# Making the right operands of the second layer's Strassen products during the first layer, by way of DRAM

## The chip, the core and the metric

The kernel runs on one core of one Trainium2 chip. The time is that of one execution on the device in microseconds (us); a run's time is that of the core. PE is TensorE (the matmuls), DVE is VectorE, ACT is ScalarE, POOL is GpSimd, and SP is SyncE, which here only issues DMAs.

## What is computed

One layer of an encoder, batch 1, 2048 positions, width 1024, all in float32. Three mixers (dilated attention, latent attention, spatial gating) and an output projection come first and are not touched. The part that matters here is the MLP behind them:

```python
x = _layer_norm(ALPHA * x + y @ w_out, ln1_g, ln1_b)
f = jnp.square(jax.nn.relu(x @ w_ff1 + b_ff1)) @ w_ff2 + b_ff2      # 1024 -> 4096 -> 1024
return _layer_norm(ALPHA * x + f, ln2_g, ln2_b)
```

## The kernel before, in words

**Numbers.** A float32 operand is split into a high part (a copy to fp32r, on ACT) and a low part (the operand less the high part, on DVE or POOL). A product is then three matmuls, high by high, low by high and high by low (`mm3`, lines 149 to 151). A page is 128 partitions by 512 floats, 256 KB.

**Strassen.** Both layers of the MLP (`feed_forward`) take blocks two by two and make seven products from sums and differences of the blocks. The products are numbered 1 to 7. Each needs a left operand (made by `left`) and a right one (made by `right`); both make the sum or difference first and split it then (`parts`, lines 1367 and 1368).

**Rounds.** A round is the seven products, 84 matmuls of 512 columns, for one pair of blocks. Rounds 0 to 31 are the first layer ("hidden rounds": two halves `hf` of the positions by 16 chunks `c` of the hidden features; left operands W from `w1`, right operands X from the normed x, made once per half). Rounds 32 to 63 are the second layer (8 blocks `c` of the hidden features by 4 groups `g` of positions; left operands H from the hidden features, right operands V from `w_ff2`, made once per block `c` and used in its four rounds). In the second layer each product ends in two additions of a PSUM bank to the result `acc` in SBUF (line 1594, on DVE).

**Order.** `feed_forward` writes the program in the order run a product of round r, prepare the operand of the same number for round r + 1 (`prepare`), and loads what round r + 2 needs at the end of round r. A scheduler then orders each engine's queue. In the hidden rounds PE takes the products of round k in the order 1, 5, 2, 6, 3, 7, 4, with 7 of round k standing between 1 and 5 of round k + 1, and 4 between 5 and 2 of round k + 1. So product 2 of round k + 1 starts right behind product 4 of round k, and its left operand (W..2h and W..2l; the name holds half, chunk and product) is made on ACT and POOL just ahead of it.

**V before.** For each block `c`, four double pages of `w_ff2` are loaded (line 1572), and during the last round of the block before, `right` makes V: 8 subtractions, four on POOL and four on DVE (line 1428), 14 high parts on ACT and 14 low parts on DVE (line 1368). The V pages are held once, not twice: a page is written anew as soon as the product that read it is done. For block 0 this happens in hidden round 31.

**DMA.** All these DMAs are issued by SP, in its queue's order; each waits for its operands and for the DMA eight places ahead of it to have landed.

Of the kernel before, what the change touches and what calls it, by code (L numbers as in the profile page):

```python
# [94 lines left out]
def f(ap):  # L95
    return ap.bitcast(F32)
# [3 lines left out]
def hybrid_layer(ctx: ExitStack, tc: tile.TileContext, a):  # L100
# [33 lines left out]
    y_d = [[dt_([P, TB], f"y_d{i}_{b}") for b in range(NB)] for i in range(8)]  # L134
    x1T_d = [dt_([P, KD, S // 2], f"x1T_d{i}") for i in range(2)]
    xb_d = [dt_([TB, DM], f"xb_d{i}") for i in range(NB)]
    hid_d = [[dt_([P, 4, TB], f"hid_d{i}_{j}") for j in range(NB)] for i in range(8)]

    def hp(k):
# [1213 lines left out]
    def feed_forward(done):  # L1353

        with ExitStack() as es:
# [31 lines left out]
            def load_page(kind, src, nm, view=None):  # L1387
                t = page(kind, nm)
                dma(t if view is None else t.rearrange("p (k c) -> p k c", c=view), src)
                return t  # L1390
# [27 lines left out]
            def right(B, n, nm, late):  # L1418

                out = {}  # L1420

                def put_(p, raws):
                    kind = {1: "X1", 2: "X2", 4: "xr" if n == 2 else "X4"}.get(p, "X")
                    out[p] = [parts(kind, raws[i], f"{nm}{p}{i}", dve) for i in range(n)]

                def sub(o, x, y):
                    for i in range(n):
                        (dve if i % 2 else pool).tensor_tensor(o[i], x[i], y[i], op=ALU.subtract)  # L1428

                def p5():  # L1430
                    sub(B[0, 0], B[0, 1], B[0, 0])
                    put_(5, B[0, 0])

                def p6():
                    sub(B[0, 0], B[1, 1], B[0, 0])
                    put_(6, B[0, 0])

                def p7():
                    sub(B[0, 1], B[1, 1], B[0, 1])
                    put_(7, B[0, 1])  # L1440
                    late()

                def p4():
                    sub(B[0, 0], B[1, 0], B[0, 0])
                    put_(4, B[0, 0])

                return out, {1: lambda: put_(1, B[0, 0]), 5: p5, 6: p6, 3: lambda: put_(3, B[1, 1]), 7: p7,
                             2: lambda: put_(2, B[1, 0]), 4: p4}
# [18 lines left out]
            def hidden_round(hf, c, big, bf1):  # L1467
# [60 lines left out]

                return load, preps, run

            def second_rounds():


                acc, late, gb = {}, [], {}
                rounds = []
                for c in range(DFF // TB):
                    big = {}
                    for g in range(4):
                        rounds.append(second_round(c, g, big, acc, late, gb))
                return rounds, late  # L1540

            def second_round(c, g, big, acc, late, gb):
                nm = f"{c}_{g}"
                end = c == DFF // TB - 1
                A, bks = {}, {}
                H, prep = left(A, "wc", f"H{nm}", (3, 7, 2, 4), {2: "ht", 4: "ht"})
                preps = [prep]
                if g == 0:
                    big["B"] = {}
                    big["W"], bp = right(big["B"], 2, f"V{c}", lambda: None)  # L1550
                    preps.insert(0, bp)
                if c == 0 and g == 0:

                    order = []
                    for q in range(4):
                        for j, n in ((0, 0), (1, 1), (0, 1), (1, 0)):
                            order += [(4 * q + 2 * j + i, n) for i in range(2)]

                    def residual(lo, hi):
                        for m, n in order[lo:hi]:  # L1560
                            acc[m, n] = load_page({0: "X1", 20: "X2", 24: "X4"}.get(lo, "X"), xb_d[m // 4][(m % 4) * P:(m % 4 + 1) * P, n * TB:(n + 1) * TB], f"acc{m}{n}")
                    preps.append({p: (lambda i=i: residual(4 * i, 4 * i + (8 if i == 6 else 4)))
                                  for i, p in enumerate((1, 5, 6, 3, 7, 2, 4))})

                def load():
                    for j in range(2):
                        for k in range(2):
                            A[j, k] = load_page("wr", hid_d[c][g][:, 2 * k:2 * k + 2, 256 * j:256 * j + 256], f"A{nm}{j}{k}", 256)
                    if g == 0:
                        for k, b in ((0, 0), (0, 1), (1, 1), (1, 0)):  # L1570
                            r0 = (4 * c + 2 * k) * P
                            big["B"][k, b] = [load_page("xr", a["w_ff2"][r0 + i * P:r0 + (i + 1) * P, b * TB:(b + 1) * TB],
                                                        f"B{c}{k}{b}{i}") for i in range(2)]
                    if end and g == 1:
                        gb["g"] = row_pages("xr", a["ln2_g"], "g2")
                        gb["b"] = row_pages("xr", a["ln2_b"], "b2")

                sums, norms = {}, []

                def run(p, bk):  # L1580
                    for i in range(2):
                        if p in FRESH:
                            bks[bk, i] = (first_bank(f"o{nm}{p}{i}") if bk == "a" else
                                          bank(dict(b=("av", "st")[i], c="st")[bk], f"o{nm}{p}{i}"))
                        ps = bks[bk, i]
                        for kt in range(2):
                            cols = slice(256 * kt + P * i, 256 * kt + P * i + P)
                            w = big["W"][p][kt]
                            mm3(ps, H[p][0][:, cols], H[p][1][:, cols], w[0], w[1], p in FRESH and kt == 0, kt == 1, True)
                        j, n = {1: (0, 0), 5: (1, 1), 6: (0, 1), 3: (0, 1), 7: (1, 1), 2: (0, 0), 4: (1, 0)}[p]  # L1590
                        m = 4 * g + 2 * j + i
                        t = acc[m, n]
                        if not end or p not in (3, 7, 2, 4):
                            dve.tensor_tensor(t, ps, t, op=ALU.add)  # L1594
                            continue
                        if g == 3:

                            dve.tensor_tensor(t, ps, t, op=ALU.add)
                            if m not in sums:
                                sums[m] = sm.tile([P, 2, 6], F32, tag="stats", name=f"fs{m}", bufs=4)  # L1600
                            dve.bn_stats(sums[m][:, n], t)
                        else:
                            if m not in sums:
                                sums[m] = sm.tile([P, 2], F32, tag="sums", name=f"fs{m}", bufs=4)
                            dve.scalar_tensor_tensor(t, ps, 1.0, t, ALU.mult, ALU.add, accum_out=sums[m][:, n:n + 1])  # L1605
                        if p == ((3 if j == 0 else 4) if end and g == 3 else 2 if j == 0 else 4):
                            def store(m=m):
                                for n in range(2):
                                    dma(a["out"][m * P:(m + 1) * P, n * TB:(n + 1) * TB], acc[m, n])
                            norms.append(layer_norm([acc[m, 0], acc[m, 1]], sums[m], gb["g"], gb["b"], f"b{m}", lambda nm: page("sx", nm), store, dve if m >= 14 else pool,  # L1610
                                                    sums[m] if g == 3 else None))
                    if norms and (len(norms) == 4 or g == 3):
                        n = len(norms)
                        for i in range(n + 2):
                            late.extend(norms[i - k][k] for k in range(3) if 0 <= i - k < n)
                        norms.clear()

                return load, preps, run
# [41 lines left out]
                prepare(2, p)  # L1660
            rounds[3][0]()
            final = len(rounds) - 1
            for r in range(2, len(rounds)):
                for i, (p, bk) in enumerate(LAST if r == final else ORDER):
                    rounds[r][2](p, bk)
                    prepare(r + 1, (LAST if r + 1 == final else ORDER)[i][0])
                    for _ in range(3 if r == final else 2):
                        if late and (i < 6 or r == final):
                            e = late.pop(0)
                            if e:  # L1670
                                e()
                if r + 2 < len(rounds):
                    rounds[r + 2][0]()
# [76 lines left out]
```

## Time and profile before

| | us |
|---|---|
| median of 3 runs | 2957.93 (2956.33 to 2963.31) |
| the profiled execution, its own time | 2963.83 |
| its span, first to last instruction | 2962.0 |
| PE busy | 2809.6 (95%) |
| DVE busy | 2035.9 (69%) |
| POOL busy | 1567.3 (53%) |
| ACT busy | 1334.3 (45%) |

The hidden rounds take the stretch from about 1625 to 2265 us of the span, the second layer from there to the end. Busy time is the sum over instructions; a busy PE can still be waiting for nothing and run at half its clock, which the granted clock shows (1.00 is the full 2.4 GHz). A row of waits tells which engine waited at which line for which instruction, the sum, how often, and the longest.

### The profile page before, as it was taken

How to read it: one execution, taken by the hardware profiler on the slowest of the kernel's cores; microseconds unless marked ns; L12 is line 12 of the kernel's file. 1: busy time of each engine (PE TensorE's matmuls, PEld its weight loads, DVE VectorE, ACT ScalarE, POOL GpSimd, SP SyncE). 2: the span in 40 equal slices, each digit the busy share in tenths (PEclk: the TensorE clock that was granted, in tenths of full speed). 3: DMA queues.
4: the chain of work that ended last, by engine and by line, in shares of the span. 5: the costliest groups of instructions: out<-in, count | busy, mean ns of one | idle time of the engine just before them, and what ended most of it. 6: DMA issues, size and time to landing. Idle time of an engine off the chain costs nothing. (4 is left out here: it accounts for less than half of the span.)

```text
span 2962.0 us, 38261 instructions
## 1 busy us (share of the span) xinstructions
PE 2809.6 (95%) x12562; PEld 2284.3 (77%) x12562; DVE 2035.9 (69%) x3543; ACT 1334.3 (45%) x2510; POOL 1567.3 (53%) x1227
## 2 busy tenths in 40 slices
PE   9999998999899999998999999989999999999996
PEld 7776877888778878886778788868887777777774
DVE  4246877676787878778677733473337777778899
ACT  4225555556555555456544533443434332232243
POOL 0115556546544554458665544554446666565667
PEclk9999999999999999999999999999999999999998
DMA  5335333235122443114374532333326222222222
GB/s 170 122 130 180 109 112 107 97 116 122 35 55 58 88 86 79 36 37 130 101 234 145 167 107 107 107 128 107 114 104 228 84 69 78 78 86 79 78 72 96
DMA packets 255567, 313.99 MB, mean 106 GB/s; under 512 B 79516, under 2 KB 145788, under 8 KB 254844
## 3 DMA queue, kind: packets, MB, share of 16 engines
q1 hardware_dynamic: 242056, 295.82, 33.2%
q10 hardware_dynamic: 13312, 15.73, 1.5%
q8 instruction: 99, 1.62, 0.2%
q14 instruction: 100, 0.82, 0.1%
HBM read 209.72 MB, written 98.60 MB: 104 GB/s over the span
## 5 line engine op out<-in xcount | busy, mean ns | idle before, releaser
L621 POOL TENSOR_TENSOR pl<-pr,ph 128x512 fp32r<-128x512 f32 x384 | 506.8, 1334 | 438.8 <-ACT ph L619 327.7
L1594 DVE TENSOR_TENSOR acc<-o,acc 128x512 f32<-128x512 f32 x416 | 275.0, 683 | 108.3 <-PE o L151 106.1
L618 ACT ACTIVATE pr<-st 128x512 f32<-128x512 f32 x384 | 228.3, 598 | 182.6 <-PE st L613 171.0
L594 DVE TENSOR_REDUCE m<-mx 128x1 f32<-128x512 f32 x384 | 256.5, 682 | 74.2 <-PE mx L593 72.3
L640 DVE TENSOR_TENSOR acp<-acp,pr 128x512 f32<-128x512 f32 x312 | 215.9, 692 | 53.8 <-ACT pr L618 49.2
L619 ACT ACTIVATE ph<-st 128x512 fp32r<-128x512 f32 x384 | 222.9, 598 | 20.8 <-PE av L647 13.8
L611 PE MATMUL st<-QH,KL 96*128 96x512 f32 x384 | 162.3, 423 | 13.9 <-ACT ph L619 13.1
L593 PE MATMUL mx<-KH,QH 96*128 96x512 f32 x384 | 159.0, 436 | 16.4 <-DVE m L594 9.7
L648 PE MATMUL av<-pl,VV 128*128 128x512 f32 x384 | 161.2, 420 | 6.5 <-POOL pl L621 6.4
L647 PE MATMUL av<-ph,VV 128*128 128x512 f32 x384 | 158.1, 412 | 0.8 <-DVE y L662 0.7
L612 PE MATMUL st<-QL,KH 96*128 96x512 f32 x384 | 154.7, 403 | 0.0
L613 PE MATMUL st<-QH,KH 97*128 97x512 f32 x384 | 154.3, 408 | 0.0
L875 DVE CUSTOM_DVE_ANT_0 jk<-amx,bias 128x256 bf16<-128x256 f32 (+2 forms) x288 | 103.8, 360 | 19.9 <-PE amx L870 10.1
L1521 DVE TENSOR_TENSOR t<-t,h 128x512 f32<-128x512 f32 x32 | 22.0, 686 | 138.4 <-PE h L151 127.0
L1010 PE MATMUL aav<-apr,v 128*65 128x128 f32 (+3 forms) x624 | 113.0, 324 | 2.9 <-DVE acc L998 1.0
L954 PE MATMUL ast<-QB,KB 65*128 65x256 f32 (+1 forms) x288 | 103.6, 372 | 4.9 <-DMA QB<-amr 3.9
L953 PE MATMUL ast<-QA,KA 128*128 128x256 f32 (+1 forms) x288 | 106.3, 374 | 0.9 <-DVE tt L976 0.6
L979 ACT ACTIVATE apr<-tt 128x192 f32<-128x192 f32 (+2 forms) x180 | 77.6, 467 | 62.5 <-PE aav L1010 57.5
L1010 PEld LDWEIGHTS aav<-apr,v 128*65 128x65 f32 x624 | 81.2, 140 | 31.5 <-issue 1.6
L593 PEld LDWEIGHTS mx<-KH,QH 96*128 96x128 f32 x384 | 75.5, 201 | 37.5 <-DVE m L594 16.3
L149 PE MATMUL po<-woh,y 128*128 128x512 f32 x256 | 102.8, 403 | 1.0 <-ACT xT L1266 1.0
L151 PE MATMUL po<-wol,y 128*128 128x512 f32 x256 | 101.9, 400 | 0.7 <-DVE wol L1207 0.7
(9022 smaller groups left out, 8706.3 us busy)
## 6 DMA issues: line engine op xcount, KB each, us to landing
A<-in_w SPq DMA_DIRECT2D x128, 256.0 KB, 2.7
hid_d<-t SPq DMA_DIRECT2D x128, 256.0 KB, 2.7
A<-hid_d SPq DMA_DIRECT2D x128, 256.0 KB, 2.7
B<-in_w_ff SPq DMA_DIRECT2D x64, 256.0 KB, 3.5
xr<-in_xT SPq DMA_DIRECT2D x56, 256.0 KB, 3.5
wr<-in_wf SPq DMA_DIRECT2D x48, 256.0 KB, 3.1
yr<-y_d SPq DMA_DIRECT2D x64, 128.0 KB, 2.3
xt<-in_x SPq DMA_DIRECT2D x32, 256.0 KB, 3.7
```

Source lines behind the costliest of these rows:

```text
L593: pe.matmul(ps, s["QH"][0:96, qt * P:(qt + 1) * P], kh[0:96, kc * TB:(kc + 1) * TB], start=True, stop=True)
L594: dve.tensor_reduce(s["m16"][:, qt, kc:kc + 1], ps, AX.X, ALU.max)
L611: pe.matmul(st, kl[0:96, kk], s["QH"][0:96], start=True, stop=False)
L612: pe.matmul(st, kh[0:96, kk], s["QL"][0:96], start=False, stop=False)
L618: act.activation(pr, st, AF.Exp, scale=SC)
L619: act.activation(ph, st, AF.Exp, scale=SC)
L621: pool.tensor_tensor(pl, pr, f(ph), op=ALU.subtract)
L640: dve.tensor_tensor(s["ac"], old, pr, op=ALU.add)
L647: pe.matmul(s["av"], VV[h][:, kt], ph, start=(kt == 0), stop=False)
L648: pe.matmul(s["av"], VV[h][:, kt], pl, start=False, stop=(kt == NT - 1))
L1010: pe.matmul(s[key][0:65, c0:c0 + w], s["V"][p][:, units[u][2] + j], pr[:, a0:a0 + w], start=(first[key] == i), stop=(last[key] == i), skip ...
L1594: dve.tensor_tensor(t, ps, t, op=ALU.add)
```

## The change

The V operands of all eight blocks are made during the hidden rounds, 16 items of one block `c` and one half `i` each, and stored to DRAM as finished high and low pages (`vv_d`, 14 pages an item). The second layer loads these pages into the V pages as they come free, and makes none of them. An item loads 4 pages of `w_ff2`, makes 4 subtractions (two on POOL, two on DVE), 7 high parts on ACT and 7 low parts on DVE, and stores 14 pages. The program takes it in nine steps, one behind each product, 63 steps from round 2 on and 81 from round 17 on.

```diff
+    vv_d = [[dt_([P, 14, TB], f"vv_d{c}{i}") for i in range(2)] for c in range(DFF // TB)]
...
+            SECOND = (1, 5, 6, 4, 2, 7, 3)
+            def second_right():
+                done_ = []
+                def store():
+                    while done_:
+                        dst, t = done_.pop(0)
+                        dma(dst, t)
+                for c in range(DFF // TB):
+                    for i in range(2):
+                        B = {}
+                        for k, b in ((0, 0), (1, 0), (0, 1), (1, 1)):
+                            r0 = (4 * c + 2 * k + i) * P
+                            B[k, b] = load_page("xr", a["w_ff2"][r0:r0 + P, b * TB:(b + 1) * TB], f"V{c}{i}{k}{b}")
+                        yield
+                        for n, p in enumerate(SECOND):
+                            raw = B[{1: (0, 0), 5: (0, 0), 6: (0, 0), 4: (0, 0), 2: (1, 0), 7: (0, 1), 3: (1, 1)}[p]]
+                            x = {5: (0, 1), 6: (1, 1), 4: (1, 0), 7: (1, 1)}.get(p)
+                            if x:
+                                (pool if p in (5, 4) else dve).tensor_tensor(raw, B[x], raw, op=ALU.subtract)
+                            h = page("xr", f"V{c}{i}{p}h", F32R)
+                            act.copy(h, raw)
+                            l = page("xr", f"V{c}{i}{p}l", F32R) if n < 3 else raw.bitcast(F32R)
+                            dve.tensor_tensor(l, raw, f(h), op=ALU.subtract)
+                            store()
+                            done_.extend([(vv_d[c][i][:, 2 * n], h), (vv_d[c][i][:, 2 * n + 1], l)])
+                            yield
+                        store()
+                        yield
...
-                    big["B"] = {}
-                    big["W"], bp = right(big["B"], 2, f"V{c}", lambda: None)
-                    preps.insert(0, bp)
+                    big["W"] = {}
+                    def fetch(p):
+                        kind = {1: "X1", 2: "X2", 4: "xr"}.get(p, "X")
+                        n = 2 * SECOND.index(p)
+                        big["W"][p] = []
+                        for i in range(2):
+                            hl = [page(kind, f"V{c}_{p}{i}{x}", F32R) for x in "hl"]
+                            for x in range(2):
+                                dma(hl[x], vv_d[c][i][:, n + x])
+                            big["W"][p].append(hl)
+                    preps.insert(0, {p: (lambda p=p: fetch(p)) for p in SECOND})
...
-                    if g == 0:
-                        for k, b in ((0, 0), (0, 1), (1, 1), (1, 0)):
-                            r0 = (4 * c + 2 * k) * P
-                            big["B"][k, b] = [load_page("xr", a["w_ff2"][r0 + i * P:r0 + (i + 1) * P, b * TB:(b + 1) * TB],
-                                                        f"B{c}{k}{b}{i}") for i in range(2)]
...
+            ahead = second_right()
+            quota = [63, 81]
             for r in range(2, len(rounds)):
                 for i, (p, bk) in enumerate(LAST if r == final else ORDER):
                     rounds[r][2](p, bk)
                     prepare(r + 1, (LAST if r + 1 == final else ORDER)[i][0])
+                    if (2 <= r < 12 or 17 <= r < 31) and quota[r // 16]:
+                        quota[r // 16] -= 1
+                        next(ahead)
```

The scheduler decides where the moved work stands. Three places follow.

**DVE, last round of block 0 in the second layer, where V of block 1 was made.** `acc..` are the additions from PSUM, `H..l` and `V..l` low parts of left and right operands, `B..` subtractions for V. Before:

```order
L1368 TENSOR_TENSOR H1_01l_22444<-A1_000_22395,H1_01h_22443 128x512
L1594 TENSOR_TENSOR acc141_21948<-o0_350_22447,acc141_21948 128x512
L1428 TENSOR_TENSOR B1001_22405<-B1011_22409,B1001_22405 128x512
L1368 TENSOR_TENSOR V150l_22466<-B1000_22403,V150h_22465 128x512
L1594 TENSOR_TENSOR acc151_21950<-o0_351_22455,acc151_21950 128x512
L1368 TENSOR_TENSOR H1_05l_22476<-H1_0s_22473,H1_05h_22475 128x512
L1428 TENSOR_TENSOR B1011_22409<-B1111_22413,B1011_22409 128x512
L1594 TENSOR_TENSOR acc121_21952<-o0_310_22419,acc121_21952 128x512
L1368 TENSOR_TENSOR V151l_22470<-B1001_22405,V151h_22469 128x512
L1594 TENSOR_TENSOR acc120_21944<-o0_320_22564,acc120_21944 128x512
```

The same place in the changed program:

```order
L1370 TENSOR_TENSOR H1_01l_23220<-A1_000_23187,H1_01h_23219 128x512
L1635 TENSOR_TENSOR acc141_22740<-o0_350_23223,acc141_22740 128x512
L1635 TENSOR_TENSOR acc100_22704<-o0_210_23050,acc100_22704 128x512
L1635 TENSOR_TENSOR acc110_22706<-o0_211_23058,acc110_22706 128x512
L1635 TENSOR_TENSOR acc151_22742<-o0_351_23231,acc151_22742 128x512
L1370 TENSOR_TENSOR H1_05l_23250<-H1_0s_23247,H1_05h_23249 128x512
L1635 TENSOR_TENSOR acc121_22744<-o0_310_23195,acc121_22744 128x512
L1635 TENSOR_TENSOR acc131_22746<-o0_311_23203,acc131_22746 128x512
L1370 TENSOR_TENSOR H1_06l_23277<-H1_0s_23247,H1_06h_23276 128x512
```

All 18 DVE operations for V are gone from between the additions; only additions and low parts of H are left.

**ACT and POOL, hidden round 3 of the second half, up to the left operand of product 2 of round 4.** `t61_3` and `t71_3` copy a PSUM bank after products 6 and 7, `W1_4..` are left operands of the next round. ACT before:

```order
L1513 ACTIVATE t61_3_19939<-h1_31_19887,bf1_15750 128x512
L1367 CAST W1_46h_19942<-W1_4s_19921 128x512
L1367 CAST W1_43h_19962<-W1_4s_19921 128x512
L1367 CAST W1_47h_19984<-A1_400_19879 128x512
L1513 ACTIVATE t71_3_19978<-h1_31_19887,bf1_15750 128x512
L1367 CAST W1_42h_20004<-A1_401_19881 128x512
```

ACT in the changed program:

```order
L1515 ACTIVATE t61_3_20398<-h1_31_20335,bf1_15766 128x512
L1558 CAST V505h_20754<-V5000_20693 128x512
L1369 CAST W1_46h_20401<-W1_4s_20374 128x512
L1558 CAST V506h_20780<-V5000_20693 128x512
L1369 CAST W1_43h_20426<-W1_4s_20374 128x512
L1369 CAST W1_47h_20450<-A1_400_20327 128x512
L1515 ACTIVATE t71_3_20444<-h1_31_20335,bf1_15766 128x512
L1558 CAST V504h_20807<-V5000_20693 128x512
L1558 CAST V502h_20834<-V5010_20695 128x512
L1558 CAST V507h_20860<-V5001_20697 128x512
L1558 CAST V503h_20885<-V5011_20699 128x512
L1369 CAST W1_42h_20478<-A1_401_20329 128x512
```

POOL in the changed program:

```order
L1410 TENSOR_TENSOR W1_4s_20374<-A1_401_20329,W1_4s_20374 128x512
L1556 TENSOR_TENSOR V5000_20693<-V5010_20695,V5000_20693 128x512
L1520 TENSOR_TENSOR t71_3_20444<-t71_3_20444,t51_3_20372 128x512
L1370 TENSOR_TENSOR W1_42l_20479<-A1_401_20329,W1_42h_20478 128x512
```

Six casts of an item stand among ACT's work, four of them right ahead of W1_42h, and the item's subtraction for product 4 (line 1556) stands ahead of the last two POOL operations before product 2.

**SP, the same last round of block 0 in the second layer.** `A..` are loads of left operands, `V1_..` the new loads, here for products 1 and 5 of block 1:

```order
L145 DMA V1_10h_23211<-vv_d10_142 128x512
L145 DMA V1_10l_23212<-vv_d10_142 128x512
L145 DMA V1_11h_23215<-vv_d11_143 128x512
L145 DMA V1_11l_23216<-vv_d11_143 128x512
L145 DMA A1_200_23533<-hid_d1_2_162 128x2x256
L145 DMA V1_50h_23239<-vv_d10_142 128x512
L145 DMA V1_50l_23240<-vv_d10_142 128x512
L145 DMA V1_51h_23243<-vv_d11_143 128x512
L145 DMA V1_51l_23244<-vv_d11_143 128x512
```

Each V load waits until PE has done the product that reads the page, and loads of left operands stand between them. Product 4's V loads stand earlier, for three blocks at once.

## Rows read from the trace of the kernel before

**Rows 1.** The page's busy time: us, share of the span, instructions.

```profile
PE 2809.6 (95%) x12562; PEld 2284.3 (77%) x12562; DVE 2035.9 (69%) x3543; ACT 1334.3 (45%) x2510; POOL 1567.3 (53%) x1227
```

**Rows 2.** Stretches: length, busy PE, PEld, DVE, ACT, POOL (instructions), clock, DMA share, GB/s.

```profile
1540.00:1560.00 20.00, 20.00 (x98) 16.68 (x97) 12.43 (x29) 9.93 (x25) 10.63 (x12) 1.00 0.97 306
1700.00:1800.00 100.00, 100.00 (x433) 81.05 (x433) 35.31 (x52) 39.59 (x67) 48.57 (x37) 1.00 0.31 110
2270.00:2290.00 20.00, 19.74 (x84) 15.43 (x84) 17.94 (x22) 8.37 (x15) 14.85 (x10) 1.00 1.03 366
2500.00:2600.00 100.00, 95.92 (x411) 76.78 (x410) 83.81 (x106) 32.59 (x57) 62.78 (x45) 1.00 0.22 70
```

**Rows 3.** PE's waits from 2300 to 2880 us: sum, times, longest.

```profile
PE o L149 <- DVE acc L1594: 21.6, 14, 2.5
```

**Rows 4.** Timeline of PE: start, length, instruction, idle time before it and its releaser.

```profile
2517.90 0.50 PE L149 MATMUL o<-V350h,H_05h 128*128 128x512 f32 x1 [0.80 <-DVE acc L1594]
...
2523.66 0.50 PE L149 MATMUL o<-V240h,H_34h 128*128 128x512 f32 x1 [2.48 <-DVE acc L1594]
...
2879.31 0.50 PE L149 MATMUL o<-V730h,H_13h 128*128 128x512 f32 x1 [1.66 <-DVE acc L1594]
```

**Rows 5.** Timeline of a quiet hidden round (round 4), and the first reader of W_52l on PE.

```profile
1710.11 0.69 ACT L1513 ACTIVATE t<-h,bf 128x512 f32<-128x512 f32 x1
...
1729.56 0.69 ACT L1513 ACTIVATE t<-h,bf 128x512 f32<-128x512 f32 x1
1731.83 0.62 ACT L1367 CAST W_52h<-A 128x512 fp32r<-128x512 f32 x1 [1.59 <-PE h L150]
...
1723.73 0.69 DVE L1515 TENSOR_TENSOR t<-t,h 128x512 f32<-128x512 f32 x1 [1.76 <-PE h L151]
...
1732.53 1.29 POOL L1368 TENSOR_TENSOR W_52l<-A,W_52h 128x512 fp32r<-128x512 f32 x1 [0.92 <-ACT W_52h L1367]
...
L150 PE MATMUL h<-X020h,W_52l x1: 389/389/389, 1734.8 to 1734.8; 128*128 128x512 f32 x1
```

**Rows 6.** 2300 to 2860 us: DVE by line; DVE at L1368; DVE and POOL at L1428.

```profile
L1594 DVE TENSOR_TENSOR acc<-o,acc 128x512 f32<-128x512 f32 x382 | 252.4, 683 | 105.8 <-PE o L151 103.7
L1428 DVE TENSOR_TENSOR B<-B,B 128x512 f32<-128x512 f32 x28 | 33.4, 1193 | 0.0
...
2300.00:2860.00 560.00, 185.31 (x181) 1.00 0.24 76
...
2300.00:2860.00 560.00, 33.40 (x28) 39.00 (x28) 1.00 0.24 76
```

**Rows 7.** Timeline of hidden round 31: the first and last operation for V0, POOL's last steps, PE.

```profile
2246.58 0.62 ACT L1367 CAST V010h<-B 128x512 fp32r<-128x512 f32 x1
...
2280.72 1.78 DVE L1368 TENSOR_TENSOR V071l<-B,V071h 128x512 fp32r<-128x512 f32 x1
...
2257.03 1.65 POOL L1428 TENSOR_TENSOR B<-B,B 128x512 f32<-128x512 f32 x1 [1.84 <-PE h L150]
2258.64 1.71 POOL L1368 TENSOR_TENSOR W_152l<-A,W_152h 128x512 fp32r<-128x512 f32 x1
...
2260.40 0.79 PE L150 MATMUL h<-X120h,W_152l 128*128 128x512 f32 x1 [2.96 <-POOL W_152l L1368]
...
2263.55 0.40 PE L151 MATMUL h<-X122l,W_152h 128*128 128x512 f32 x1
```

**Rows 8.** DMA issues: line, operation, count, size, us from issue to landing.

```profile
B<-in_w_ff SPq DMA_DIRECT2D x64, 256.0 KB, 3.5
...
acc<-xb_d SPq DMA_DIRECT2D x32, 256.0 KB, 5.3
```

**Rows 9.** Timeline of ACT and DVE at the start of the hidden rounds.

```profile
1651.36 0.62 ACT L1367 CAST X041h<-x 128x512 fp32r<-128x512 f32 x1
1651.88 0.62 ACT L1367 CAST X022h<-x 128x512 fp32r<-128x512 f32 x1
...
1655.64 1.20 DVE L1368 TENSOR_TENSOR X022l<-x,X022h 128x512 fp32r<-128x512 f32 x1
```

## The prediction

> **What bounds the kernel now.** I read the busy times first, then the stretches, then PE's waits in the stretch that the change is about, and last the timelines of single places. The page says that PE is busy for 95% of the span [rows 1]; so only PE's gaps can be won, some 150 us over the whole kernel, and most of them lie in parts that the change does not touch. The stretches show two different regimes [rows 2]. In the hidden rounds (1700 to 1800) PE is busy without a break, DVE for 35 of 100 us, ACT for 40, POOL for 49, and DMA has a share of 0.31. In the second layer (2500 to 2600) PE is busy for 95.9 and DVE for 83.8. PE's waits name what ends there: 21.6 us of waiting for line 1594, the additions on DVE that free a PSUM bank, and for nothing else [rows 3]. The timeline says when: a gap of 0.80 and one of 2.48 us, close together, once in each block, where the last round of a block meets the first of the next [rows 4]. That is the round in which V is made.
>
> The reason is a sum on DVE. A round lasts 19.45 us (from one copy of a bank to the same copy a round later [rows 5]). In a plain round of the second layer DVE has 14 additions of 0.683 and 3 low parts, together under 13 us. In the round that makes V it has 18 operations more. Line 1368 takes 185.31/181 = 1.02 us each and line 1428 1.19 [rows 6], so these are 14 x 1.02 + 4 x 1.19 = 19.0 us, and with 12.6 for the rest 31.6 us of work for 19.45. What neighbouring rounds don't absorb, PE waits for.
>
> **What the change takes away.** (a) Seven such meetings. The waits are 21.6 us; the last one, 1.66 us at 2879, lies inside block 7 [rows 4], where no V is made, and stays. Gain **19.9 us**. With 17 DVE operations left a round (the DVE rows of the order), DVE is under 13 of 19.45 us, so no addition is late. (b) Hidden round 31. PE waits 2.96 us for W_152l, which POOL reaches late because a subtraction for V0 of 1.65 us stands ahead of it [rows 7]. Behind that gap eight matmuls take 2263.55 - 2260.40 = 3.15 us; at the full clock, 19.45/84 = 0.232 us each, they take 1.85. Gain 2.96 + 1.30 = **4.3 us**. Both bounds for (a) and (b) are near: they are PE's own idle time, and nothing else can be won there.
>
> **What it adds in the second layer.** 28 V loads a block for 8 loads of `w_ff2`. A page is released when its product is done and read a round later, 19.45 us, and a load at full traffic lands after 5.3 us [rows 8]. A round with 28 V loads and some 5 others moves 33 x 0.262 MB = 8.7 MB; at the 366 GB/s that the trace shows [rows 2] that is 23.6 us, 4 more than a round. So the last pages come some 4 + 5 us after their release, 10 ahead of use. I take **nothing**. Behind a V load that waits for PE on SP stand only loads of H's operands, one round or more early. Bounds: 0, and 7 x 5.3 = 37 us if each block waited for one landing.
>
> **What it adds in the hidden rounds.** The order puts about one item into each round, faster than the program's nine steps for seven products: 16 of the 32 rounds carry one. The engines' sums for such a round: ACT 0.40 x 19.45 + 7 x 0.62 = 12.1 us; POOL 0.49 x 19.45 + 2 x 1.39 = 12.3 (1.39 is 39.00/28, POOL's half of line 1428 [rows 6]); DVE 0.353 x 19.45 = 6.9, plus 9 x 1.02 = 9.2, is 16.1, and 18.7 if its own eight SBUF operations also slow from 0.69 to 1.02. All are under 19.45, so no engine is the bound, but the cover on DVE is thin. What counts then is the place with the least lead. That is product 2: ACT writes W_52h at 1731.83, POOL W_52l from 1732.53 to 1733.82, and PE reads it at 1734.8 [rows 5]. The lead is **1.0 us**.
>
> For the round in the order's second place I add up the new chain on the clock of [rows 5]. It starts when DVE adds product 3, 1723.73. Five DVE operations follow up to the low part for product 6 of the item, with a cast between: 5 x 1.02 + 0.62 + 0.7 = 6.4, to 1730.1. POOL's subtraction for product 4, 1.39: 1731.5. The casts V504h to V503h, four at a spacing of 0.52 [rows 9], then W1_42h, 0.62: 1734.2. W1_42l on POOL, 1.29 to 1.71: 1735.5 to 1735.9. That is 0.7 to 1.1 us too late. Without the waits for DVE, four casts behind 1729.56 would delay W1_42h by 0.4 us only, and nothing would be lost. In nine of the 16 rounds POOL's subtraction for product 4 stands ahead of that low part as here; in the other seven it stands behind it or far earlier, and at most two casts stand there: I take 1.0 us for the nine and 0.3 for the seven, **11.1 us**. Below: 0, if operations meet as seldom as in a quiet round. Above: the nearest row of a hidden round with V work in it is round 31, where both items of V0, made from 2246.58 to 2280.72 (1.75 rounds), cost 2.96 us [rows 7], 1.5 an item: 24 us. I stay between, nearer to the chain, since the order around product 2 differs from round 31's.
>
> DVE's 1.78 us for a low part of V [rows 7] against a flat 0.683 for the additions [rows 6] shows what makes V's operations dear: both their inputs lie in SBUF, while an addition has one in PSUM. The Trainium skill says the same in SBUF — State Buffer, Who interferes with whom: a VectorE instruction with two SBUF inputs contends with a GpSimd instruction that reads SBUF, and the later one blocks until the first is done. This rule speaks against the change, which moves 144 such operations next to POOL's work on the operands that PE waits for; the third rival is that rule at its full price.
>
> **Two edges.** At the start, V001h stands on ACT between X041h and X022h [rows 9] and waits for a load issued behind those for X; a load of this kind lands after 3.5 us [rows 8], and X022l on DVE has 3.1 us in hand (1655.64 less 1652.5). I take 2 us, bounds 0 and 5. Where the second half begins, an item mixes into the making of X: 1 us, bounds 0 and 2. Together **3 us**.
>
> **Sum.** -19.9 - 4.3 + 11.1 + 3 = -10.1 us, against the profiled execution's 2963.8: 2953.7. That execution stands 5.9 us above the median of the runs, 2957.9; carried over, **2947.8 us**, 0.34% less. A measurement of this kernel can tell about 0.3%, 8.9 us, from no change, so the forecast is just beyond it. At the lower bounds of all costs: 2957.9 - 24.2 = 2933.7. At the upper bounds of the hidden rounds and the edges: + 24 + 7 - 24.2, 2964.7.
>
> **Rivals.** First, **the gain is given back in the hidden rounds**: product 2 is late by about 1.5 us in every item's round. For it: round 31 did just that. Against it: there, two subtractions stood ahead. Time: 2957.9 - 24.2 + 24 + 3 = 2960.7; with 1 us a round 2953. Both within 0.3%.
>
> Second, **DMA becomes the bound of those rounds**. SP's order holds 24 to 27 DMAs in 13 of them, where it held 8; 26 are 6.8 MB in 19.45 us, 350 GB/s. The trace has 366 at a share of 1.03, and 306 at a share of 0.97 [rows 2]. At 306, 26 take 22.3 us, 2.8 over the round; in 13 rounds that is 37 us: 2957.9 - 24.2 + 37 + 3 = 2973.7. From 323 GB/s downwards (26 in 21.1 us, 1.6 over the round, 21 us in 13) it takes back the whole gain. Against it: the row of 306 lies in another stage, the one of 366 in the rounds next to these, where the same 256 KB pieces move.
>
> Third, on the other side too, **DVE becomes the bound of those rounds**, when V's operations wait for a whole POOL operation each, at 1.78 us: 6.9 + 9 x 1.78 = 22.9 us a round, 3.5 over, 56 us in 16 rounds: 2957.9 - 24.2 + 56 + 3 = 2992.7. It decides once a moved operation takes more than (19.45 - 6.9)/9 = 1.39 us in the mean. Against it: 1.02 and 1.19 in the second layer, with POOL busy for 63 of 100 us there.
>
> Fourth, **V comes late**: PE's wait for DVE becomes one for a V load at each block. At 2 to 5.3 us for each of the seven: 2961.9 to 2985 with the hidden rounds' cost as forecast. Against it: the lead of ten us worked out above.
>
> **How the numbers follow.** The forecast, transitions won and hidden rounds costing 0 to 12 us, has 0.52; the first rival 0.28, nearly all of it within 0.3%; the second 0.09, of which 0.02 within; the third 0.07; the fourth 0.04, half within. That makes faster 0.52, same 0.31, slower 0.17. The range runs from the lower bounds, rounded to 2933, over the first rival and the sum's upper bounds to 2968; beyond it lie the dear ends of the last three rivals and what I overlooked.
>
> **What would show it.** In the second layer, PE's waits for the additions fall from 21.6 to about 2 us, DVE's busy share there to some 60%. The wait for W_152l in round 31 is gone. In the hidden rounds PE has short waits, around a us, at product 2, put down to POOL's low part of W, one in most rounds with an item, and DMA has a share of 0.9. The forecast is wrong if PE waits there for several us a round, with DVE (third rival) or DMA (second) busy throughout, or if PE's waits in the second layer name V.

## The result, and the profile after

The changed kernel takes **2990.07 us** (median of 6 runs, 2980.84 to 2997.22), the kernel before 2960.23 (6 runs on the same chip, 2955.43 to 2966.05): a ratio of 1.0102, 95% interval 1.0089 to 1.0116. It is 1% slower. The forecast was 2947.8, and the range ended at 2968.

The profiled execution of the changed kernel has a span of 2994.6 us, 32.6 more than before. Its busy times, beside [rows 1]:

```profile
PE 2827.7 (94%) x12562; PEld 2296.2 (77%) x12562; DVE 2066.5 (69%) x3543; ACT 1332.9 (45%) x2510; POOL 1577.3 (53%) x1227
```

The counts are those of before: V's 144 operations on DVE and 32 on POOL were moved, none was added. Still DVE is busy for 30.6 us longer and POOL for 10. That the move made operations longer is the first thing to see here.

Stretches of the changed kernel, with the columns of [rows 2]: two with items in the hidden rounds, the second layer, and all hidden rounds as one.

```profile
1700.00:1800.00 100.00, 86.84 (x348) 67.54 (x347) 76.23 (x79) 47.31 (x85) 57.34 (x39) 0.95 0.80 277
2000.00:2100.00 100.00, 87.19 (x350) 68.27 (x350) 78.27 (x82) 45.30 (x81) 56.33 (x37) 0.95 0.79 268
2300.00:2900.00 600.00, 600.00 (x2585) 485.40 (x2584) 359.64 (x520) 144.09 (x238) 329.58 (x251) 1.00 0.51 168
...
1621.50:2329.90 708.40, 651.42 (x2675) 515.14 (x2673) 474.21 (x536) 330.58 (x582) 390.83 (x264) 0.96 0.64 221
```

The hidden rounds of the kernel before as one stretch (both reach from PE's first matmul on the left operand of product 1 of round 0 to that of round 32):

```profile
1623.50:2270.10 646.60, 627.95 (x2676) 505.33 (x2674) 309.92 (x403) 278.17 (x480) 327.85 (x235) 0.99 0.35 121
```

PE's first matmuls of block 7 in the kernel before (count, lengths, first and last start; the later start is taken as the block's):

```profile
L149 PE MATMUL o<-V710h,H_01h x2: 393/394/394, 2838.0 to 2842.1; 128*128 128x512 f32 x2
```

The same row of the changed kernel, over all eight blocks:

```profile
L151 PE MATMUL o<-V_10h,H_01h x16: 391/397/404, 2329.9 to 2880.6; 128*128 128x512 f32 x16
```

From these the 32.6 us divide as follows:

| stage | before | after | difference |
|---|---|---|---|
| up to the hidden rounds | 1623.5 | 1621.5 | -2.0 |
| hidden rounds | 646.6 | 708.4 | **+61.8** |
| second layer, to block 7 (2842.1, 2880.6) | 572.0 | 550.7 | **-21.3** |
| from there to the end (2962.0, 2994.6) | 119.9 | 114.0 | -5.9 |

From 2300 to 2900, nearly all of it second layer, PE is busy for 600.00 of 600 us. In the hidden rounds it loses 38 us more than before in waits (708.4 - 651.4 against 646.6 - 628.0) and 23.5 us in matmuls that take longer, at a mean clock of 0.96 in place of 0.99. Its waits in the hidden rounds of the changed kernel, the first four rows, largest sum first (who waited at which line for what, sum, times, longest):

```profile
PE h L151 <- ACT t L1515: 24.5, 8, 6.5
PE h L152 <- POOL W_52l L1370: 4.6, 2, 3.2
PE h L152 <- POOL W_152l L1370: 3.5, 1, 3.5
PE h L152 <- POOL W_62l L1370: 3.2, 2, 2.3
```

The two largest rows of the kernel before, in its hidden rounds:

```profile
PE h L149 <- ACT t L1513: 8.2, 3, 6.6
PE h L150 <- POOL W_152l L1368: 6.4, 2, 3.5
```

So not all of these waits are new, and two places share what is. One is that of the forecast, product 2: its rows stand apart by chunk, and all those for W..2l together are 19.6 us in 13 waits, with 4.0 more for W..2h on ACT, where the kernel before had 6.4: 17.2 us more. The other is product 4, which has nearly all of the first row: it adds to the bank that product 7 left, and waits until ACT has copied it to t. The sum was 8.2 us and is 24.5, 16.3 more; the longest, 6.5, was there before. All other waits grew by 5.0 us. One of the new waits of product 4, from 2025 to 2038, in the timelines of DVE, POOL, ACT and PE (start, length, instruction, idle time before it):

```profile
2025.70 1.78 DVE L1560 TENSOR_TENSOR V405l<-V,V405h 128x512 fp32r<-128x512 f32 x1
2027.51 1.67 DVE L1556 TENSOR_TENSOR V<-V,V 128x512 f32<-128x512 f32 x1
...
2030.90 1.78 DVE L1560 TENSOR_TENSOR V406l<-V,V406h 128x512 fp32r<-128x512 f32 x1
...
2025.18 1.75 POOL L1375 TENSOR_TENSOR W_3s<-A,A 128x512 f32<-128x512 f32 x1
2026.89 1.74 POOL L1414 TENSOR_TENSOR A<-A,A 128x512 f32<-128x512 f32 x1
...
2032.76 1.28 POOL L1556 TENSOR_TENSOR V<-V,V 128x512 f32<-128x512 f32 x1 [0.63 <-DVE V406l L1560]
...
2034.08 0.62 ACT L1558 CAST V404h<-V 128x512 fp32r<-128x512 f32 x1 [1.28 <-DMA A<-in_w]
2034.60 0.61 ACT L1558 CAST V402h<-V 128x512 fp32r<-128x512 f32 x1
...
2036.68 0.68 ACT L1515 ACTIVATE t<-h,bf 128x512 f32<-128x512 f32 x1
...
2030.36 0.39 PE L153 MATMUL h<-X173l,W_17h 128*128 128x512 f32 x1
...
2037.41 0.79 PE L151 MATMUL h<-X140h,W_14h 128*128 128x512 f32 x1 [3.85 <-ACT t L1515]
```

Read it from below. PE ends product 7 at 2030.75; t is copied at 2036.68, because the casts V404h to V403h stand ahead of it on ACT. V404h waits (the row names a DMA, but POOL's subtraction ends at 2034.04, just before it starts), that subtraction waits for V406l on DVE, and V406l comes behind operations of 1.67 and 1.78 us. Above stand the lengths: DVE's low part takes 1.78 while POOL is at work and POOL's steps 1.75 and 1.74. A quiet step of POOL takes 1.29 [rows 5], and a low part on DVE, made from two SBUF pages as V's are, 0.69 with no POOL operation beside it, in round 4 of the kernel before:

```profile
1727.71 0.69 DVE L1368 TENSOR_TENSOR W_53l<-W_5s,W_53h 128x512 fp32r<-128x512 f32 x1 [1.84 <-ACT W_53h L1367]
```

### The profile page after: what moved, and what is told of

It is laid out like the page before. It is cut to its first block, busy times and chain, and to the rows that moved or that the text cites. A ratio compares the mean times of both kernels' runs of the same rounds, so it can differ in the third digit from the quotient of the medians.

```text
span 2994.6 us, 39099 instructions
## 1 busy us (share of the span) xinstructions
PE 2827.7 (94%) x12562; PEld 2296.2 (77%) x12562; DVE 2066.5 (69%) x3543; ACT 1332.9 (45%) x2510; POOL 1577.3 (53%) x1227
## 5 line engine op out<-in xcount | busy, mean ns | idle before, releaser
L1635 DVE TENSOR_TENSOR acc<-o,acc 128x512 f32<-128x512 f32 x416 | 282.4, 689 | 213.4 <-PE o L153 208.1
L151 PE MATMUL po<-woh,y 128*128 128x512 f32 x256 | 102.9, 403 | 0.5 <-ACT xT L1268 0.5
L152 PE MATMUL po<-woh,y 128*128 128x512 f32 x256 | 102.2, 399 | 0.0
```

The lines of the kernel that those rows point to most:

```text
L151: pe.matmul(ps, wh, xh, start=first, stop=False, skip_group_check=reopen)
L152: pe.matmul(ps, wl, xh, start=False, stop=False, skip_group_check=reopen)
```

## The experiments

Theory 1: V's operations themselves cost the time, by their length and by stretching their neighbours (1a), or by their places in the queues of ACT and POOL (1b). Theory 2: it is the DMAs. All ratios are to the kernel before on the same chip; the runs are from several chips, on which the kernel before has medians of 2960.2 to 2964.5, so a difference of times between chips is good to some 4 us only. "Hidden" is the stretch of 646.6 us before, in the profiled run.

| run | us | ratio, 95% interval | hidden |
|---|---|---|---|
| changed kernel | 2990.07 | 1.0102 (1.0089 to 1.0116) | 708.4 |
| e1_gain_only | 2929.78 | 0.9887 (0.9871 to 0.9904) | 643.3 |
| e2_no_stores | 2995.02 | 1.0106 (1.0084 to 1.0129) | 708.9 |
| e3_dma_only | 2936.92 | 0.9918 (0.9898 to 0.9938) | 651.1 |
| e4_subs_dve | 2990.59 | 1.0093 (1.0067 to 1.0119) | 711.9 |
| e5_short_ops | 2931.51 | 0.9902 (0.9885 to 0.9919) | 646.8 |
| e6_no_chain | 2978.22 | 1.0059 (1.0041 to 1.0077) | 690.0 |
| e8_one_input | 2952.56 | 0.9969 (0.9956 to 0.9982) | 666.4 |
| e9_psum_input | 2943.52 | 0.9948 (0.9929 to 0.9968) | 657.7 |

**Gain and cost apart.** e1_gain_only: no `next(ahead)`, and in `fetch`

```diff
-                                dma(hl[x], vv_d[c][i][:, n + x])
+                                s = 14 * i + n + x
+                                dma(hl[x], x1T_d[s // 16][:, s % 16 // 2, s % 2 * TB:(s % 2 + 1) * TB])
```

> Leaves out the making of V altogether; the second layer loads as many pages of other data (x1T) in V's place. Step (a) and (b) of the prediction alone, with the 28 loads a block. If the gain came as forecast (24.2 us, V loads at nothing): about 2936, 0.992 of before, with PE busy for 100 us of each 100 in the second layer, and the whole excess of the changed kernel, some 54 us, is the price of making V in the hidden rounds. If the loads of V pages cost something themselves or the transitions give less: 2945 or more.

2929.78: the gain is 33 us, 9 more than forecast, and the loads of V pages cost nothing. So making V in the hidden rounds costs 2990.07 - 2929.78 = 60 us (64 by the ratios).

**DMA or engines.** e2_no_stores has the same `fetch` and drops the stores in `store`; e3_dma_only keeps loads and stores:

```diff
-                            x = {5: (0, 1), 6: (1, 1), 4: (1, 0), 7: (1, 1)}.get(p)
...
-                            dve.tensor_tensor(l, raw, f(h), op=ALU.subtract)
+                            h = l = raw
```

> Makes V in the hidden rounds as the changed kernel does, but does not store it (224 stores of 256 KB fewer); the second layer loads other data. Theory 1 (V's operations on POOL, DVE and ACT, their length and their places in the queues, cost the hidden rounds their time): at most 10 us less than the changed kernel, 2980 or more. Theory 2 (pages come free late because stores stand in the DMA queues, and w1's and w_ff2's loads land late, 4.4 and 4.9 us): most of the 54 us gone, 2945 or less.

> The reverse: loads four pages of w_ff2 an item and stores 14 pages, but leaves out the subtractions, high and low parts (the loaded pages are stored as they are). Theory 1: 2936 to 2945. Theory 2: 2970 or more, with PE waiting for operands whose loads land late.

Without the stores nothing is won (2995.02). With the DMAs alone 7 of the 60 us remain (2936.92). Theory 2 falls.

**POOL's queue.** e4_subs_dve:

```diff
-                                (pool if p in (5, 4) else dve).tensor_tensor(raw, B[x], raw, op=ALU.subtract)
+                                dve.tensor_tensor(raw, B[x], raw, op=ALU.subtract)
```

> V's two subtractions of an item that stood on POOL (products 5 and 4) go to DVE. If POOL's queue (a subtraction of V ahead of t7's addition and of product 2's low part) is what makes PE wait: 15 to 30 us less than the changed kernel, about 2965. If the length of the operations on DVE and POOL side by side is what counts, or ACT waiting for V's subtractions wherever they run: within 8 us of the changed kernel, or slower, as DVE gets 2 x 1.2 us a round more.

2990.59, no change in the sum, but not at each place: PE's waits for product 2's low part fall from 19.6 to 11.7 us, and those for t rise from 24.5 to 31.7. This suggests that what POOL's queue gave back, the same subtractions on DVE took again.

**Length or places.** e5_short_ops:

```diff
+                                w = slice(0, 32)
+                                (pool if p in (5, 4) else dve).tensor_tensor(raw[:, w], B[x][:, w], raw[:, w], op=ALU.subtract)
...
+                            w = slice(0, 32)
+                            dve.tensor_tensor(l[:, w], raw[:, w], f(h)[:, w], op=ALU.subtract)
+                            l = h
```

> V's subtractions and low parts work on 32 of 512 columns; the casts on ACT, the loads and the 14 stores of an item stay whole (the high page is stored in the low part's place), and every wait between the engines stays. Theory 1a (what costs is the length of V's operations with two SBUF inputs, and that they stretch DVE's and POOL's other ones: squares from 0.69 to 1.0 us, t7's addition from 1.29 to 1.72): nearly the whole excess gone, 2945 or less, and squares and t7's additions near 0.69 and 1.3 again. Theory 1b (queue places alone: V's casts stand on ACT ahead of t7's copy and of product 2's high part and wait for POOL and DVE, however short those operations are): 2970 or more.

e6_no_chain:

```diff
+                                (pool if p in (5, 4) else dve).tensor_tensor(junk[p in (5, 4)], B[x], raw, op=ALU.subtract)
...
+                            l = h
+                            dve.tensor_tensor(junk[0], raw, B[0, 1], op=ALU.subtract)
```

> As many whole operations for V on the same engines as in the changed kernel, but none waits for one on another engine: casts read the loaded pages, subtractions and low parts read loaded pages and write to one spare page of their engine, 14 stores an item go from the cast's pages. V's contents are thus not made. Theory 1a (stretching alone): within 15 us of the changed kernel, 2975 or more. Theory 1b (the chain from subtraction to cast to low part across three queues): 2950 or less. Both needed, stretching making V late and the chain handing the delay on to ACT: 2950 to 2965.

With short operations and every wait in place 2931.51, within 2 us of the gain alone (4 by the ratios): the queue places cost next to nothing by themselves, and so do e5's DMAs. Of the two lengths that were expected back near the quiet ones, t7's addition came back (1.294 us from 1700 to 1830), the squares did not (0.904). With whole operations and no waits among them 2978.22: the chain adds 12 us, and 48 of the 60 come without it. PE still waits 19.2 us at product 2 and 15.1 for t there.

**What makes them long.** Two runs keep e4's eleven DVE operations an item, their waits and their 512 columns, and change what they read. e8_one_input:

```diff
+                                dve.tensor_scalar(raw, B[x], 1.0, None, op0=ALU.mult)
...
+                            dve.tensor_scalar(l, f(h), 1.0, None, op0=ALU.mult)
```

> As the run with V's subtractions on DVE, but each of V's eleven DVE operations an item is a copy of one page by tensor_scalar (one SBUF input in place of two, the same 512 columns, queues, casts, stores; the contents of V are not made). Theory 1a in its narrow form (DVE's operations with two SBUF inputs and POOL's operations shut each other out): the operations take 0.7 us or less throughout, t7's additions on POOL stay at 1.29, and the time is 2930 to 2950. If it is DVE's busy time or the number of operations in the queues, whatever they read: within 12 us of the run with two inputs, 2990.6.

e9_psum_input (the line that frees a bank for it is left out here):

```diff
+                            spare.append(bank("ac", "spare"))
+                            act.copy(spare[0], B[0, 0])
...
+                                dve.tensor_tensor(raw, spare[0], B[x], op=ALU.subtract)
...
+                            dve.tensor_tensor(l, spare[0], f(h), op=ALU.subtract)
```

> As the run with V's subtractions on DVE (2990.6), with the same eleven DVE operations an item over 512 columns, the same waits, casts and stores, but one input of each is a bank of PSUM that is filled once (V's contents are not made; the bank is taken from those of the hidden rounds' products 1 and 6, which keep three). The additions that read PSUM took a flat 0.683 us beside busy POOL, so these should too. If DVE and POOL shut each other out only where DVE's inputs are all in SBUF: t7's additions back to 1.29 to 1.35, and 2930 to 2950, though DVE does as many operations of the same length. If it is DVE's time or the number of operations that counts: 2975 or more.

e9 settles it: 2943.52, 47 us less than e4 (43 by the ratios) for the same number of operations. The hidden rounds of e4:

```profile
1617.50:2329.40 711.90, 652.60 (x2674) 515.61 (x2673) 475.61 (x568) 330.16 (x582) 343.96 (x232) 0.96 0.64 220
```

V's subtractions there, in the groups by line (count, busy us, mean ns, idle before):

```profile
L1556 DVE TENSOR_TENSOR V<-V,V 128x512 f32<-128x512 f32 x64 | 71.8, 1128 | 6.2 <-DMA V<-in_w_ff 4.5 <-DMA hid_d<-t 1.1
```

The same two of e9:

```profile
1614.50:2272.20 657.70, 632.79 (x2676) 504.67 (x2675) 426.30 (x568) 330.38 (x582) 328.35 (x232) 0.98 0.68 238
```

```profile
L1559 DVE TENSOR_TENSOR V<-spare,V 128x512 f32<-128x512 f32 x64 | 43.6, 682 | 18.9 <-DMA V<-in_w_ff 13.5 <-DMA A<-in_w 3.3 <-issue 2.2
```

568 operations on DVE and 232 on POOL in both. V's subtractions take 0.682 us in place of 1.128, and POOL's operations, the same in both, 328 us in place of 344. DVE and POOL hold each other up when both work on SBUF, and a tensor_tensor of DVE that takes one input from PSUM is free of it.

The squares and t7's addition in e9, the first from 1621 to 2263, the second from 1621 to 2270:

```profile
L1499 DVE SCALAR_TENSOR_TENSOR t<-t 128x512 f32<-128x512 f32 x93 | 86.3, 929 | 18.9 <-POOL t L1520 17.4 <-DMA hid_d<-t 1.3
```

```profile
L1520 POOL TENSOR_TENSOR t<-t,t 128x512 f32<-128x512 f32 x31 | 42.4, 1367 | 68.2 <-ACT t L1515 68.2
```

The squares, which work on SBUF alone, are as long as in the hidden rounds of the changed kernel (0.929 there too), so their length is not what the 47 us are. t7's addition takes 1.367, a little over the expected 1.29 to 1.35, where the changed kernel has 1.565 and the kernel before 1.361 over all hidden rounds.

e8 came out between (2952.56), and the narrow form of the theory is wrong. The copies have one SBUF input, and are held up all the same, though POOL's steps are not (331.15 us busy in the hidden rounds, for 328.35 in e9). A step of POOL and two of them in e8's timeline:

```profile
2024.29 1.29 POOL L1406 TENSOR_TENSOR W_3s<-W_3s,A 128x512 f32<-128x512 f32 x1 [1.64 <-DVE W_35l L1370]
...
2024.30 1.57 DVE L1560 TENSOR_SCALAR V416l<-V416h 128x512 fp32r<-128x512 f32 x1
...
2028.94 0.42 DVE L1560 TENSOR_SCALAR V<-V412h 128x512 fp32r<-128x512 f32 x1
```

1.57 us for the one that starts 0.01 us after POOL's step, 0.42 for the one with no POOL operation beside it. They gain because a copy alone is short, not because it is free. The Trainium skill (SBUF — State Buffer, Who interferes with whom) says that a copy or tensor_scalar too can contend with GpSimd, when it runs in a two-port mode. The 1.57 beside the 0.42 agrees; which mode the copies ran in, no run here shows.

**The same work elsewhere.** If the hidden rounds have no room for V, the second layer may: after the change DVE is busy there for 60 of 100 us. v1_second makes block 0's V in rounds 29 and 30 and the others' in the first three rounds of the block before; v2_spread makes block 0's as the kernel before did and spreads the rest:

```diff
+            def steps(s):
+                return 0 if s < 0 else (s + 1) * 18 // 21 if s < 21 else 18 + (s - 20) * 18 // 28
+
+            def made(r, i):
+                s = 7 * (r - 32) + i
+                return min(steps(s), 126) - min(steps(s - 1), 126)
```

v3_paced10 and v3_paced8 take V's high pages from those of H as well:

```diff
-                            h = page("xr", f"V{c}{i}{p}h", F32R)
+                            h = page("ht", f"V{c}{i}{p}h", F32R)
```

> The same work in another place: V of block 0 in hidden rounds 29 and 30, V of blocks 1 to 7 during the first three rounds of the block before, in the second layer. The gain alone measured 2929.8; two items in hidden rounds at the 4 us each of the changed kernel are 8. In the second layer DVE had 60 of 100 us busy in the changed kernel, and 18 operations more in three rounds bring it to about 60 + 19/77.8 = 84. If DVE absorbs that because it is spread: 2938 to 2950, faster than both kernels. If additions become late again as in the kernel before, or POOL's operands for H: 2960 or more.

> V of block 0 made in round 31 as in the kernel before, V of blocks 1 to 7 in the second layer ahead of their blocks (18 steps over 21, then over each 28 products). The first try of this kind measured 2955.5; two items of block 0 cost it 16 us in the first rounds of the second half, where round 31 cost 4.3 us before, and PE's waits for the additions were 2.05 us a block. Expected 2940 to 2948. If the port is as full in the second layer with V spread as in the hidden rounds: 2955 or more.

> As v2_spread, with V's high pages taken in turn with the pages of H for products 2 and 4 (10 of them), so that V's work cannot run more than some 1.3 rounds ahead of its place in the program. The two items of a block then take 20 to 30 and 20 additions' time in place of 25 to 37 and 10. If bunching is what makes the additions late: the waits of 2.05 us a block gone, 5 to 10 us under v2_spread. If not: the same within 4 us.

> As v3_paced10 with 8 pages in turn in place of 10: V's items at an even 20 to 24 additions each. The same 8 pages serve t in the hidden rounds, which use 5 a round. If even spreading counts and t does not need the other two pages: 2 to 6 us under v3_paced10. If t needs them: PE waits for t's copies in all hidden rounds, 2960 or more.

| run | us | ratio, 95% interval |
|---|---|---|
| v1_second | 2955.54 | 0.9984 (0.9969 to 0.9999) |
| v2_spread | 2943.85 | 0.9938 (0.9917 to 0.9959) |
| v3_paced10 | 2942.40 | 0.9934 (0.9909 to 0.9959) |
| v3_paced8 | 2940.24 | 0.9928 (0.9906 to 0.9951) |

v1 missed its range: the scheduler moved block 0's two items up to the first rounds of the second half, where X is still made, and its hidden rounds take 659.2 us, 16 more than e1's. v2 came out as expected, and the last three beat both kernels. v3_paced10 is 1.5 us under v2_spread, where bunching was to be worth 5 to 10, and v3_paced8 2.2 under that; the intervals overlap, so whether pacing adds anything is open. From 2270 to 2860 PE waits for the additions thus, in v2_spread:

```profile
PE o L151 <- DVE acc L1644: 8.0, 12, 1.2
```

and in v3_paced8:

```profile
PE o L151 <- DVE acc L1644: 4.3, 7, 1.8
```

Is V held up less in the second layer? The additions and V's subtractions on DVE in v2_spread, from 2270 to 2840:

```profile
L1644 DVE TENSOR_TENSOR acc<-o,acc 128x512 f32<-128x512 f32 x395 | 257.1, 682 | 66.7 <-PE o L153 65.1
L1556 DVE TENSOR_TENSOR V<-V,V 128x512 f32<-128x512 f32 x28 | 31.9, 1139 | 12.3 <-POOL V L1556 12.1
```

and in the hidden rounds of the changed kernel:

```profile
L1556 DVE TENSOR_TENSOR V<-V,V 128x512 f32<-128x512 f32 x32 | 35.8, 1123 | 18.5 <-POOL V L1556 15.2 <-DMA V<-in_w_ff 3.1
```

In v2_spread it is not, though the run costs 14 us and not 60; in v3_paced8 the subtractions take 0.887. The additions keep their 0.682 us; whether that, or a longer lead of the operands, makes the place cheap was not tried.

## Why the prediction was wrong

**(a) and (b), the gains: right in kind, too small.** The waits for the additions are gone; up to block 7 the second layer is 21.3 us shorter, for 19.9 forecast. That nothing else could be won there was wrong: the last block is 5.9 us shorter too. PE's first 40 us of block 7, before and after:

```profile
2842.10:2882.10 40.00, 36.12 (x153) 28.09 (x151) 39.19 (x68) 16.40 (x34) 25.78 (x20) 1.00 0.28 93
```

```profile
2880.60:2920.60 40.00, 40.00 (x174) 32.40 (x173) 34.29 (x66) 15.85 (x32) 26.08 (x23) 1.00 0.35 123
```

3.88 us of the 5.9 are waits for the additions in these 40 us, among them the 1.66 at 2879 that the forecast took to stay. What shortens the rest was not tried. Round 31: e1's hidden rounds are 3.3 us shorter than before, for 4.3.

**V loads at nothing: right.** PE is busy without a break from 2300 to 2900 in the changed kernel, and e1 has the same loads.

**The hidden rounds at 11.1 us, bounds 0 to 24: the step that failed.** With the edges the forecast charged 14.1 us to these rounds; measured are 61.8 and the 3.3 won in round 31, 65. The 61.8 are 17.2 us of waits at product 2, 16.3 for t, 5.0 elsewhere and 23.5 of slower matmuls. Three things in that step failed:

- What a moved operation does to the others. Its own price was right: from 2000 to 2200 DVE's operations at L1560 and L1556 (the first two rows, busy us and count) take (54.55 + 19.49)/(57 + 17) = 1.00 us, for 1.02 and 1.19 forecast. But POOL's operations were kept at the quiet round's length in the sum, and the chain was laid on the times of that round. Product 2 was the right place, and it still cost 17.2 us and its slower matmuls for 11.1.
- The place. "The place with the least lead" was taken to be product 2 alone. Product 4 waits for ACT's copy of t7, with only product 5 between, and the waits for t grew by 16.3 us. ACT's casts had been counted by their length, not by what they wait for.
- The clock. Round 31's gap was given its slow matmuls; the new gaps were not, and 23.5 of the 61.8 us are those.

The stretches of the changed kernel for DVE at L1560, then at L1556 (length, busy, count, clock, DMA share, GB/s):

```profile
2000.00:2200.00 200.00, 54.55 (x57) 0.94 0.80 279
...
2000.00:2200.00 200.00, 19.49 (x17) 0.94 0.80 279
```

And its groups of the squares on DVE and of t7's addition on POOL, from 1700 to 1830:

```profile
L1499 DVE SCALAR_TENSOR_TENSOR t<-t 128x512 f32<-128x512 f32 x18 | 17.7, 984 | 0.1
...
L1520 POOL TENSOR_TENSOR t<-t,t 128x512 f32<-128x512 f32 x6 | 10.3, 1713 | 5.0 <-ACT t L1515 5.0
```

The same two in the kernel before:

```profile
L1497 DVE SCALAR_TENSOR_TENSOR t<-t 128x512 f32<-128x512 f32 x21 | 14.4, 685 | 8.9 <-POOL t L1518 8.9
...
L1518 POOL TENSOR_TENSOR t<-t,t 128x512 f32<-128x512 f32 x7 | 9.0, 1293 | 23.1 <-ACT t L1513 23.1
```

Both became longer, but the squares did so in e5 and e9 too, which cost 2 and 14 us. What goes with the time is the length of V's own operations and of POOL's: what two engines share has to be charged to both.

The upper bound, 1.5 us an item from round 31, was no bound: measured are 65/16 = 4.1. It left out the slow matmuls of its own row (1.30 us), and it came from one round with items in it, where here many follow one another; what that adds was not tried.

**The rivals.** The first had the right place, product 2, at 24 us, and neither product 4 nor the clock. The second (DMA) is refuted by e2 and e3, at 7 us. The fourth did not happen. The third gave 2992.7, close to 2990.07, but not for its reason: it had DVE full, and decided from 1.39 us an operation. The operations take 1.00, and DVE is busy for 76 to 78 of 100. Its cause, DVE and POOL waiting for each other, is the right one; what it lacked is that no engine need be full for that, when an operand with little lead stands behind longer operations (48 us in e6), or behind casts that wait for them (the other 12). It got 0.07 on the lengths of V's own operations in the second layer alone.

**Open.** e9 still takes 14 us more than e1. The DMAs alone took 7 in e3 and 2 to 4 in e5; the squares are still long in e9, and it has a PSUM bank less. What each is worth was not tried.

## What to carry to other kernels

Before moving work into an idle stretch of an engine, ask what that engine shares: DVE was busy there for 35 and POOL for 49 of 100 us, and still they were in each other's way. Charge the stretching to the operations on both engines, and then look at every place where something that PE waits for stands in a queue behind the moved work. The same work can be cheap in another place: spread over the second layer, where most of DVE's operations are additions from PSUM, making V cost 10 us (v3_paced8 less e1; 12 by the ratios) in place of 60.

## What was not expected of the hardware

- In e8 a one-input copy on DVE of 0.42 us took up to 1.57 beside POOL; in e9 a tensor_tensor with one input in PSUM stayed at 0.67 to 0.69 through all hidden rounds.
- Beside DVE operations with two SBUF inputs the stretching goes both ways: POOL's 1.29 became 1.74 to 1.75, and DVE's 0.69 became 1.78.
- Waits of PE cost more than their length: 38 us more of them came with 23.5 us of slower matmuls, at a mean clock of 0.96 in place of 0.99.
